# Seven-product stages with an earlier preparation: loads, weight sums, stores and operand splits in another order

## The chip, the cores and the metric

The kernel runs on one core of a Trainium2 chip. TensorE (PE, with its weight load PEld) multiplies, VectorE (DVE), ScalarE (ACT) and GpSimd (POOL) work element by element, and SyncE (SP) issues nearly all the DMAs. Each engine works its own instructions off in order, and so does the queue of SP: an instruction that waits holds up all that stands behind it on its engine. The metric is the device time of one execution in microseconds, of which the median of several runs counts; a profiled execution stands beside it.

## The reference

One layer of an encoder: an input projection into attention and state-space channels, attention, a bidirectional state-space scan, a GLU, an output projection with residual, and a gated embedding with a last norm. The part that the change is about comes behind the attention:

```python
glu = y_ssm @ w_glu[i] + b_glu[i]
y_ssm = glu[..., :D_SSM] * jax.nn.sigmoid(glu[..., D_SSM:])
y_ssm = y_ssm * jax.nn.silu(gate_s)
h = h + jnp.concatenate([y_attn, y_ssm], axis=-1) @ w_out[i]
gate = jax.nn.sigmoid(rms_norm(h, norm_ple[i]) @ w_ple_gate[i])
h = h + gate * (p[i] @ w_ple_proj[i])
return rms_norm(h, norm_final)
```

All matrices are 1024 or 2048 wide, there are 1024 tokens, and everything is float32.

## The kernel before

Every float32 operand is split into a high part H and a low part L (`split`, L306 on: ACT writes H with a cast, L310, DVE writes L with a subtraction, L311), and one product block takes three matmuls of 128 x 512: H times H, H times L, L times H.

Three **stages** follow the attention: stage 0 is the GLU projection (`u_glu`), stages 1 and 2 are the attention half and the state-space half of the output projection (`u_out`). Each has 8 **units** of two 128-wide output tiles. A unit computes its 2 x 2 block product by a scheme with seven block **products** instead of eight: 7 products x 4 blocks of k x 3 matmuls = 84 matmuls of 128 x 512. This costs additions on both sides:

- On the weight side four raw blocks A11, A12, A21, A22 (tiles `sraw`, 6 buffers, loaded by `sw_dma`) give S1 = A21 + A22 and S2 = S1 - A11 (tiles `wraw`), A11 - A21 and A12 - S2 in place. These four sums per unit run on POOL (`sw_sum`, L436). `sw_prep` splits the weights of one product into `wH`, `wL` (4 buffers each). `sw_next` does so ahead of use: before the matmuls of product g it prepares up to product g + 2.
- On the operand side `t_make` forms four sums of the stage's 1024-token inputs, k by k, on POOL (L1127 to L1133), in a background thread: loads to `zz` and `t4` (tile `t` in the trace), 20 steps of waiting, four subtractions, three steps, stores to scratch `d_t`. `put_product` then loads the 28 operand tiles `st` of the next stage during the last unit of a stage, four behind each product, since the 33 large buffers leave only five free beside a full set. Each load is followed some steps later by its split (`fill`, ACT then DVE), one per step.
- On the output side the seven sums are folded into tiles `cx`. `u_out` loads two tiles of 512 KB (x or the sum so far, L1238) at the start of its unit, adds products held in `tz` to them on POOL (L1242), and adds the product in PSUM on DVE in `done` (L1245). In stage 2 each finished half is also squared on ACT and summed on POOL into `xsq` (L1253, L1254). `later` stores the two tiles (L1183). There are four `cx` buffers, that is two units.

The order of everything is the order in which the code issues it (`tc.manual_schedule`). A **step** is one `tick`: four in each product, one behind the three matmuls of a k block. Each tick advances every background thread once and issues at most one waiting fill:

```python
for g in list(self.bgs):
    ...next(g)...
if self.fq and self.fq[0][0] <= self.nt:
    self.fill(*self.fq.pop(0)[1:])
```

Behind the stages the gate (`gate`) multiplies by `w_ple_gate` and `w_ple_proj` in two halves of the tokens; `h_rstd` forms the norm for it, `finish` scales and stores the output of a half.

## Time and profile before

| what | value |
|---|---|
| median of 3 runs | 2205.79 us (2204.56 to 2208.52) |
| the profiled execution | 2209.37 us, span 2207.6 us |
| PE busy | 2093.2 us, 95% of the span, 10140 matmuls |
| PEld busy | 1725.1 us, 78% |
| DVE busy | 1484.1 us, 67% |
| POOL busy | 961.1 us, 44% |
| ACT busy | 798.6 us, 36% |
| DMA | 296.48 MB, mean 134 GB/s |

The span counts from the first to the last instruction; the execution's own time is 1.8 us longer. Busy shares are averages over parts with different limits. A busy PE need not run at its peak: the granted clock and the distance from one matmul's start to the next tell that. The stages lie between 1226 and 1763 us of the span, the gate behind them.

### The profile page before, as it was taken

The numbers are of one execution on the slowest core, as the hardware profiler recorded it, in microseconds if no ns is written. First come the engines' busy times: TensorE is split into PE (matmuls) and PEld (weight loads), VectorE is DVE, ScalarE is ACT, GpSimd is POOL, SyncE is SP. The second block draws the span as 40 slices with busy tenths as digits, with TensorE's granted clock in tenths as the row PEclk, the third lists the DMA queues.
The fourth block names the chain that finished last, engine by engine and source line by source line (L and its number), as shares of the span: only waits on it lengthen the run. The fifth ranks groups of instructions, "written<-read, shape, count | busy, mean of one in ns | idle before, by whom it ended". The sixth has DMA issues, their size and how long they took to land. (4 is left out here: it accounts for less than half of the span.)

```text
span 2207.6 us, 29212 instructions
## 1 busy us (share of the span) xinstructions
PE 2093.2 (95%) x10140; PEld 1725.1 (78%) x10140; DVE 1484.1 (67%) x2394; ACT 798.6 (36%) x1454; POOL 961.1 (44%) x837
## 2 busy tenths in 40 slices
PE   8999999999999999989999899889899899999996
PEld 6888878888878887878888678667677678877885
DVE  7654777688887887749999766736755644455334
ACT  7111222222222222457777423412433433343332
POOL 0234446555655555414212576457578711211222
PEclk9999999999999999999999999889999999999998
DMA  6323232323323223563213564665744444355433
GB/s 210 95 94 102 85 97 80 96 83 100 95 82 107 80 81 103 171 203 134 96 58 100 177 205 148 241 207 197 274 138 157 169 141 127 124 185 170 124 113 124
DMA packets 187732, 296.48 MB, mean 134 GB/s; under 512 B 28864, under 2 KB 79168, under 8 KB 187328
## 3 DMA queue, kind: packets, MB, share of 16 engines
q1 hardware_dynamic: 186432, 292.51, 41.5%
q8 instruction: 80, 1.31, 0.3%
q10 hardware_dynamic: 1152, 2.10, 0.2%
q14 instruction: 68, 0.56, 0.1%
HBM read 211.37 MB, written 77.92 MB: 131 GB/s over the span
## 5 line engine op out<-in xcount | busy, mean ns | idle before, releaser
L311 DVE TENSOR_TENSOR wL<-wraw,wH 128x512 fp32r<-128x512 f32 (+1 forms) x352 | 303.1, 878 | 368.1 <-ACT wH L310 366.3
L310 ACT CAST wH<-wraw 128x512 fp32r<-128x512 f32 (+1 forms) x352 | 205.5, 597 | 356.8 <-DMA wraw<-in_w_gate_dram 110.3
L1174 PE MATMUL pr<-st,wL 128*128 128x512 f32 x672 | 274.6, 409 | 35.3 <-DVE wL L311 35.2
L1172 PE MATMUL pr<-st,wH 128*128 128x512 f32 x672 | 268.9, 400 | 12.2 <-ACT wH L310 12.2
L1173 PE MATMUL pr<-st,wH 128*128 128x512 f32 x672 | 267.7, 398 | 0.0
L1291 PE MATMUL pg<-st,wH 128*128 128x512 f32 x512 | 203.7, 398 | 9.1 <-ACT wH L310 7.7
L1292 PE MATMUL pg<-st,wH 128*128 128x512 f32 x512 | 202.4, 395 | 0.6 <-DVE st L314 0.6
L1293 PE MATMUL pg<-st,wL 128*128 128x512 f32 x512 | 201.6, 394 | 0.7 <-DVE wL L311 0.7
L1174 PEld LDWEIGHTS pr<-st,wL 128*128 128x128 f32 x672 | 130.1, 194 | 81.7 <-DVE wL L311 55.5
L1319 POOL TENSOR_TENSOR h<-cx,tz 128x512 f32<-128x512 f32 x31 | 40.4, 1304 | 309.4 <-DVE tz L1317 309.4
L1172 PEld LDWEIGHTS pr<-st,wH 128*128 128x128 f32 x672 | 130.5, 194 | 40.7 <-ACT wH L310 15.1
L1173 PEld LDWEIGHTS pr<-st,wH 128*128 128x128 f32 x672 | 129.9, 193 | 28.2
L311 DVE TENSOR_TENSOR wL<-sraw,wH 128x512 fp32r<-128x512 f32 x120 | 119.1, 993 | 39.1 <-ACT wH L310 38.5
L1242 POOL TENSOR_TENSOR cx<-cx,tz 128x512 f32<-128x512 f32 x64 | 97.0, 1531 | 107.6 <-DVE tz L1266 45.6
L892 ACT COPY ks<-kp 16x224 f32<-16x224 f32 x32 | 10.7, 335 | 344.0 <-DVE ks L891 216.3
L1291 PEld LDWEIGHTS pg<-st,wH 128*128 128x128 f32 x512 | 97.4, 190 | 32.1 <-ACT wH L310 9.3
L1292 PEld LDWEIGHTS pg<-st,wH 128*128 128x128 f32 x512 | 97.6, 191 | 23.1 <-DVE st L314 2.5
L1293 PEld LDWEIGHTS pg<-st,wL 128*128 128x128 f32 x512 | 97.4, 190 | 22.8 <-DVE wL L311 2.5
L765 POOL TENSOR_TENSOR tab<-pa 128x512 f32<-128x512 f32 x32 | 41.3, 1292 | 156.5 <-DVE r L900 156.5
L574 PE MATMUL zga<-hH,wH 128*128 128x512 f32 x256 | 104.1, 407 | 0.0
L574 PE MATMUL zq<-hH,wH 128*128 128x512 f32 x256 | 102.8, 402 | 0.0
L574 PE MATMUL zgs<-hH,wH 128*128 128x512 f32 x256 | 102.5, 400 | 0.0
(370 smaller groups left out, 5362.1 us busy)
## 6 DMA issues: line engine op xcount, KB each, us to landing
wraw<-in_w_in_dram SPq DMA_DIRECT2D x144, 256.0 KB
wraw<-in_w_gate_dram SPq DMA_DIRECT2D x128, 256.0 KB
sraw<-in_w_out_dram SPq DMA_DIRECT2D x64, 256.0 KB
st<-d_t SPq DMA_DIRECT2D x48, 256.0 KB
sraw<-in_w_glu_dram SPq DMA_DIRECT2D x32, 256.0 KB
cx<-in_xT_dram SPq DMA_DIRECT2D x16, 512.0 KB
d_p<-cx SPq DMA_DIRECT2D x16, 512.0 KB
cx<-d_p SPq DMA_DIRECT2D x16, 512.0 KB
```

The costliest lines, as they stand in the source:

```text
L310: nc.scalar.copy(H, src)
L311: nc.vector.tensor_tensor(L, src, H.bitcast(F32), ALU.subtract)
L574: nc.tensor.matmul(ps[h], H[:, kk, :], rH[:, s], start=(k == 0), stop=False)
L765: gp.tensor_tensor(out, x[:, :, None, :].to_broadcast(sh), pw[:, :, :, None].to_broadcast(sh), ALU.mult)
L1172: nc.tensor.matmul(ps, H[:, k], x[0], start=(k == 0), stop=False)
L1173: nc.tensor.matmul(ps, H[:, k], x[1], start=False, stop=False)
L1174: nc.tensor.matmul(ps, L[:, k], x[0], start=False, stop=(k == 3))
L1242: nc.gpsimd.tensor_tensor(x[:, h], x[:, h], u, ALU.add)
L1291: nc.tensor.matmul(ps, H[:, k % 4], x[0], start=(k == 0), stop=False)
L1292: nc.tensor.matmul(ps, H[:, k % 4], x[1], start=False, stop=False)
L1293: nc.tensor.matmul(ps, L[:, k % 4], x[0], start=False, stop=(k == nk - 1))
L1319: eng.tensor_tensor(hp, ho, t, ALU.add)
```

## The change

- **Weights.** `sw_next` prepares up to product g + 3 instead of g + 2. The sums S1, S2 move from the split of product 1 to that of product 0, A11 - A21 from 2 to 1, A12 - S2 from 3 to 2. The loads of the next unit's first two blocks move from `sw_prep` 0 to 3, those of the other two from 4 to 5.
- **Outputs.** The thread of the next unit starts (and so loads its `cx` tiles) behind product 3 of the unit ahead of it. The addition in `done` runs as a thread (`close`), three steps behind; the stores wait 8 steps instead of 2, the last multiplication's store in `u_glu` five instead of two.
- **Operands.** Between the start of the stages and their end a fill is issued in three of five steps (`paced`). `t_make` loads and stores two tiles of 128 x 1024 where it had four of 128 x 512, waits 14 steps for its loads, and stores 8 steps behind its last subtraction; for stage 2 it begins at unit 1 of stage 1, not at unit 0.
- **Gate.** Behind the stages all threads run out before the last two operand loads; the first gate weights are loaded behind products 3 and 5 and two are split. `h_rstd` waits two steps more. In `finish` the first half's outputs go out every second step, each stored four steps later.

```diff
@@ tick
-        if self.fq and self.fq[0][0] <= self.nt:
+        if self.fq and self.fq[0][0] <= self.nt and (not self.paced or self.nt % 5 in (0, 2, 4)):
@@ sw_prep
         if i == 0:
-            self.sw_dma(u + 1, (0, 1))
-        elif i == 1:
             self.sw_sum(u, S1, A21, A22, ALU.add)
             self.sw_sum(u, S2, S1, A11, ALU.subtract)
-        elif i == 2:
+        elif i == 1:
             self.sw_sum(u, A11, A11, A21, ALU.subtract)
             del self.sr[A21]
+        elif i == 2:
+            self.sw_sum(u, A12, A12, S2, ALU.subtract)
+            del self.sr[S2]
         elif i == 3:
             del self.sr[A11]
-            self.sw_sum(u, A12, A12, S2, ALU.subtract)
-            del self.sr[S2]
+            self.sw_dma(u + 1, (0, 1))
         elif i == 4:
             del self.sr[S1]
-            self.sw_dma(u + 1, (2, 3))
         elif i == 5:
             del self.sr[A12]
-        elif i == 6:
+            self.sw_dma(u + 1, (2, 3))
+        else:
             del self.sr[A22]
@@ sw_next
-        for j in range(g, g + 3):
+        for j in range(g, g + 4):
@@ unit
-        next(thread)
         for i in range(7):
...
             thread.send(ps)
+            if i == 3 and nxt is not None:
+                next(nxt)
             hook(i)
@@ u_out
         def done(x, h, ps):
+            self.bg(close(x, h, ps))
+
+        def close(x, h, ps):
+            for _ in range(3):
+                yield
             nc.vector.tensor_tensor(x[:, h], ps, x[:, h], ALU.add)
...
-        self.bg(self.later(2, (dst[2 * m], r[0])))
+        self.bg(self.later(8, (dst[2 * m], r[0])))
         ps = yield
         done(r[1], h0, ps)
-        self.bg(self.later(2, (dst[2 * m + 1], r[1])))
+        self.bg(self.later(8, (dst[2 * m + 1], r[1])))
@@ finish
             if hf == 0:
+                self.bg(self.later(4, (self.out[n][:, self.half(hf)], hs[n])))
                 yield
-            eng = nc.scalar if hf == 1 and n % 2 else nc.sync
+                yield
+                continue
+            eng = nc.scalar if n % 2 else nc.sync
@@ back
-                if s == 2 and i == 5:
-                    self.w_end = len(self.wq)
-                    self.w_dma()
-                    self.w_dma()
-                elif s == 2 and i == 6:
-                    self.w_split()
+                    elif i == 3:
+                        self.w_end = len(self.wq)
+                        for _ in range(2):
+                            self.w_dma()
+                    elif i == 5:
+                        self.w_dma()
+                        for _ in range(2):
+                            self.w_split()
...
-                        self.bg(self.t_make(1, src, self.four_sm, 20))
-                if u == 0 and s == 1:
-                    self.bg(self.t_make(2, self.d_ms, self.four_sm, 20))
+            if u == 1 and s < 2:
+                self.bg(self.t_make(s + 1, stages[s + 1][0], self.four_sm, 14, 8))
...
-        for _ in range(3):
+        while self.bgs:
             self.tick()
```

The order on the queue of SP in stage 1, one unit while `t_make` runs. Before (`d_t`, `zz`, `t`, `d_ms` belong to `t_make`, `d_p` is the store of finished tiles, `sraw` are weight loads):

```order
L1138 DMA d_t_1_203<-zz 128x512 x2
L1138 DMA d_t_1_203<-t_13708 128x512 x2
L1124 DMA zz<-d_ms_156 128x512 x2
L1124 DMA t_13869<-d_ms_160 128x512 x2
L1183 DMA d_p_164<-cx 128x1024
L1238 DMA cx<-in_xT_dram 128x1024 x2
L1183 DMA d_p_165<-cx 128x1024
L429 DMA sraw<-in_w_out_dram 128x512 x4
```

And now:

```order
L1129 DMA zz<-d_ms_155 128x1024
L1129 DMA t_13843<-d_ms_159 128x1024
L429 DMA sraw<-in_w_out_dram 128x512 x2
L1189 DMA d_p_164<-cx 128x1024
L429 DMA sraw<-in_w_out_dram 128x512 x2
L1189 DMA d_p_165<-cx 128x1024
L1244 DMA cx<-in_xT_dram 128x1024 x2
L1144 DMA d_t_1_203<-zz 128x1024
L1144 DMA d_t_1_203<-t_13843 128x1024
```

The loads of `cx` stood directly behind `t_make`'s stores and loads and were for the unit then beginning; now they stand ahead of those stores and are for the unit behind, and the weight loads go two by two around the stores.

The order on POOL in a unit of stage 2, from the sum S1 (`wraw<-sraw`) of one unit to that of the next. Before:

```order
L436 TENSOR_TENSOR wraw<-sraw 128x512
L436 TENSOR_TENSOR wraw<-wraw,sraw 128x512
L1254 TENSOR_TENSOR xsq<-xsq,tq 128x512
L436 TENSOR_TENSOR sraw<-sraw 128x512
L1242 TENSOR_TENSOR cx<-cx,tz 128x512
L436 TENSOR_TENSOR sraw<-sraw,wraw 128x512
L1254 TENSOR_TENSOR xsq<-xsq,tq 128x512
L1242 TENSOR_TENSOR cx<-cx,tz 128x512 x3
L1254 TENSOR_TENSOR xsq<-xsq,tq 128x512 x2
```

And now:

```order
L436 TENSOR_TENSOR wraw<-sraw 128x512
L436 TENSOR_TENSOR wraw<-wraw,sraw 128x512
L1248 TENSOR_TENSOR cx<-cx,tz 128x512
L436 TENSOR_TENSOR sraw<-sraw 128x512
L1265 TENSOR_TENSOR xsq<-xsq,tq 128x512
L436 TENSOR_TENSOR sraw<-sraw,wraw 128x512
L1265 TENSOR_TENSOR xsq<-xsq,tq 128x512 x2
L1248 TENSOR_TENSOR cx<-cx,tz 128x512
L1265 TENSOR_TENSOR xsq<-xsq,tq 128x512
L1248 TENSOR_TENSOR cx<-cx,tz 128x512 x2
```

The twelve instructions are the same. S1 and S2 stood at product 6 of the unit ahead, A11 - A21 and A12 - S2 at products 0 and 1 of the unit that needs them; now all four stand at products 4, 5 and 6 of the unit ahead.

The order on ACT at the change from stage 0 to stage 1 (`st` are operand fills, `wH` weight casts). Before:

```order
L310 CAST wH<-sraw 128x512
L310 CAST st<-st 128x512 x4
L310 CAST wH<-sraw 128x512
L310 CAST st<-st 128x512 x4
L1221 ACTIVATE tz<-tz,vec 128x512
L310 CAST wH<-wraw 128x512
L310 CAST st<-st 128x512 x4
L1258 COPY tz<-pr 128x512
```

And now:

```order
L310 CAST wH<-wraw 128x512
L310 CAST st<-st 128x512 x2
L1227 ACTIVATE tz<-tz,vec 128x512
L310 CAST wH<-sraw 128x512
L310 CAST st<-st 128x512 x2
L1269 COPY tz<-pr 128x512
L310 CAST wH<-wraw 128x512
L310 CAST st<-st 128x512 x3
```

Four fills stood between two weight casts; now there are two or three, and they reach further into the first unit of the new stage.

## Rows read from the trace of the kernel before

**Rows 1.** Stretches: length, busy us (count) of PE, PEld, DVE, ACT, POOL; clock; DMA
```profile
1226.19:1394.87 168.68, 157.79 (x674) 126.12 (x673) 121.20 (x154) 59.72 (x105) 92.80 (x62) 0.99 0.58 196
1394.87:1582.44 187.57, 166.78 (x673) 131.97 (x674) 109.94 (x141) 52.98 (x96) 113.05 (x79) 0.94 0.63 215
1582.44:1762.70 180.26, 164.38 (x673) 127.52 (x671) 118.41 (x142) 67.42 (x119) 139.08 (x93) 0.96 0.51 171
1335.81:1373.89 38.08, 38.08 (x170) 31.54 (x168) 25.57 (x33) 11.51 (x20) 18.40 (x13) 1.00 0.43 144
1762.70:1786.00 23.30, 16.55 (x65) 12.21 (x65) 12.28 (x28) 9.57 (x17) 5.48 (x4) 0.85 0.51 164
```

**Rows 2.** What PE waited for, 1226 to 1786: total us, times, longest
```profile
PE pr L1174 <- DVE wL L311: 35.2, 32, 4.9
PE pr L1172 <- ACT wH L310: 12.2, 6, 2.8
PE pg L1291 <- ACT wH L310: 4.2, 1, 4.2
```

**Rows 3.** Timeline of PE, stage 1 unit 2: start, us, what, idle before
```profile
1471.18 0.72 PE L1174 MATMUL pr<-st,wL 128*128 128x512 f32 x1 [3.70 <-DVE wL L311]
...
1472.12 0.63 PE L1173 MATMUL pr<-st,wH 128*128 128x512 f32 x1
1472.55 0.63 PE L1174 MATMUL pr<-st,wL 128*128 128x512 f32 x1
```

**Rows 4.** Timeline of POOL in the same unit
```profile
1459.85 1.30 POOL L436 TENSOR_TENSOR sraw<-sraw 128x512 f32<-128x512 f32 x1
1468.09 1.26 POOL L1242 TENSOR_TENSOR cx<-cx,tz 128x512 f32<-128x512 f32 x1 [6.95 <-DMA cx<-in_xT_dram]
1469.31 1.27 POOL L436 TENSOR_TENSOR sraw<-sraw,wraw 128x512 f32<-128x512 f32 x1
```

**Rows 5.** Timeline of SP's queue in the same unit
```profile
1457.19 0.79 SPq L1138 DMA_DIRECT2D d_t<-t  x2
...
1461.34 1.65 SPq L1238 DMA_DIRECT2D cx<-in_xT_dram  x2
```

**Rows 6.** Stretches of the three stages by units, columns as in rows 1
```profile
1226.19:1250.40 24.21, 20.48 (x87) 15.39 (x85) 19.56 (x29) 12.61 (x22) 6.63 (x4) 1.00 0.63 220
1250.40:1335.81 85.41, 80.03 (x338) 63.60 (x336) 58.28 (x68) 23.24 (x40) 61.13 (x43) 0.98 0.59 198
1373.89:1394.87 20.98, 19.20 (x85) 15.59 (x84) 17.79 (x27) 12.35 (x23) 6.64 (x5) 1.00 0.74 256
1394.87:1425.64 30.77, 24.67 (x84) 18.55 (x85) 27.67 (x34) 13.41 (x25) 15.03 (x11) 0.83 0.58 208
1425.64:1524.38 98.74, 84.64 (x337) 66.25 (x336) 44.58 (x57) 18.22 (x32) 67.14 (x49) 0.93 0.61 206
...
1562.46:1582.44 19.98, 19.39 (x86) 15.62 (x85) 14.75 (x23) 11.89 (x23) 7.21 (x5) 1.00 1.02 362
1582.44:1613.40 30.96, 22.25 (x85) 16.96 (x84) 25.58 (x33) 12.82 (x25) 19.57 (x11) 0.89 0.55 196
1613.40:1736.34 122.94, 119.41 (x506) 93.22 (x505) 70.95 (x84) 41.01 (x73) 104.33 (x72) 1.00 0.46 150
1736.34:1762.70 26.36, 22.72 (x85) 17.34 (x83) 21.88 (x25) 13.60 (x23) 15.18 (x10) 0.87 0.67 239
```

**Rows 7.** Timeline of DVE, stage 2: a split beside POOL, one alone
```profile
1644.89 1.45 DVE L311 TENSOR_TENSOR wL<-wraw,wH 128x512 fp32r<-128x512 f32 x1 [1.26 <-ACT wH L310]
...
1646.86 0.68 DVE L311 TENSOR_TENSOR wL<-sraw,wH 128x512 fp32r<-128x512 f32 x1
```

**Rows 8.** Timeline of POOL, stage 2, a sum beside a split
```profile
1642.43 1.75 POOL L436 TENSOR_TENSOR sraw<-sraw,wraw 128x512 f32<-128x512 f32 x1
```

**Rows 9.** Chain that ended last: start, us, landing of a 512 KB store
```profile
1410.13 2.80 DMA d_ms<-cx
```

**Rows 10.** What PE waited for, 1990 to 2040 (second gate half)
```profile
PE pg L1291 <- ACT wH L310: 3.5, 2, 2.7
```

94 lines of the change are left out of this document (49 added, 45 removed).

## The prediction

> **What bounds the kernel now.** I read the stretches of the three stages first [rows 1]. Two units of stage 0 in which PE never idles take 38.08 us, so a unit of 84 matmuls costs 19.04 us at the full clock, and eight cost 152.3. The stages last 168.7, 187.6 and 180.3 us, that is 16.4, 35.2 and 27.9 us more: 79.5 us in all, the most that the stages can give back. The view of PE's waits [rows 2] says for what: 47.4 us are waits for the weight split (35.2 for `wL`, 12.2 for `wH`), in 38 pieces. No operand, no PSUM buffer and no raw load appears there. The rest is mostly the clock: behind a long wait matmuls start every 0.43 us [rows 3], in an undisturbed unit every 0.227 (19.04 / 84); that is 1.2 GHz where 2.4 is granted otherwise, and the granted share in stages 1 and 2 is 0.94 and 0.96 [rows 1]. If c is the mean share, 2(1 - c) of a stretch runs at half rate and half of that is lost: 0.06 x 187.6 + 0.04 x 180.3 + 0.01 x 168.7 = 20 us. Twelve more lie in the gaps around each wait. A stall that is removed thus gives back more than one and a half times its listed wait.
>
> Next, where the units lose it [rows 6]: unit 0 of stage 0, 5.2; its units 1 to 4, 85.4 - 76.2 = 9.2; the change to stage 1 (last unit and first), 51.75 - 38.1 = 13.7; units 1 to 4 of stage 1, 98.7 - 76.2 = 22.6; the change to stage 2, 12.9; units 1 to 6 of stage 2, 122.9 - 114.2 = 8.7; its last unit 7.3. This adds up to the 79.6.
>
> Last, who makes the split late. In unit 2 of stage 1 POOL stands 6.95 us in front of an addition to `cx` [rows 4] whose load SP issued at 1461.34, behind `t_make`'s store of 1457.19 [rows 5]. A weight sum (1469.31) is queued behind that addition; its split comes late, and PE waits 3.70 us at 1471.18 [rows 3]. So in units with `t_make` the bound is SP's order, passed on by POOL's order.
>
> **The change part by part.** Matmuls, splits and sums keep their number; the sum is made of waits.
>
> *Loads a pair ahead, sums and stores moved.* The `cx` loads now go out behind product 3 of the unit ahead, 10.9 us into it. They need the buffers of the unit before that, whose second store is issued nine steps of 0.68 us into the unit (6.1) and lands 2.8 us later [rows 9], at 8.9: SP does not wait. Landing 6.7 us after issue (1461.34 to 1468.09) the data are there at 17.6, and POOL wants them at 19.04 + 2.72 + 0.6 = 22.4. The cause of rows 4 goes. The sums stand two products (5.4 us) earlier, so an addition that waits no longer holds a sum that is due. Instead POOL's load comes up: in a unit of stage 2 it works 104.3 / 6 = 17.4 us [rows 6], 1.45 us each for twelve instructions, which at 19.04 leaves 1.6. While `t_make` runs (25 steps a round instead of 26, four subtractions each) it is 8 + 4 x 28/25 = 12.5 instructions, 18.1 us. It fits, barely; a lag of some 4 us is covered, since a sum is done 7 us or so ahead of its product. Upper bound of the gain in units 1 to 4 of stages 0 and 1: 31.8, all. Lower: all POOL instructions as slow as the one beside a split, 1.75 us [rows 8]; then a unit of stage 1 takes 12.5 x 1.75 = 21.9, four lose 11.4, and 20 is gained (in stage 0, with two multiplications in place of four additions, it is 10.5 x 1.75 = 18.4, no loss). The 17.4 is measured in this same mix, so I stay near the upper end and leave one wait with its restart in each stage, 4 together: **28**. In units 1 to 6 of stage 2 nothing but the lateness of the sums causes the 1.4 us a unit: upper bound 8.7; lower 12 x 1.75 = 21.0 against 20.5 now, minus 3; I take **7.7**. What is late next there is nothing that I can see before POOL itself.
>
> The pages know a stricter rule for this place. In the rows a subtraction on DVE takes 0.68 us alone and 1.45 beside POOL [rows 7], POOL's 1.26 alone [rows 4] and 1.75 beside DVE [rows 8]. The Trainium skill, "SBUF — State Buffer", section "Who interferes with whom", has a DVE instruction with two SBUF inputs and a GpSimd instruction that reads SBUF take turns, one blocking the other for its whole length. By the rule a unit of stage 2 would hold 12 x 1.28 + 7 x 0.68 = 20.1 us of turns, one of stage 1 with `t_make` 20.8; the two terms would be 31.8 - 4 x 1.8 = 25 and 6 x 0.4 = 2.3, and the sum 53.6, that is 2152. The trace's 17.4 us, blocked time included, says that most turns are lost by DVE.
>
> *The deeper preparation.* There are still four `wH` and `wL`, so the cast for product g + 3 must wait until PE has left product g - 1. Behind it on ACT and DVE are queued fills, squares and the additions from PSUM; these wait for PE's latest products anyway, and PE needs the split three products, 8.2 us, later. Cost nothing as long as ACT and DVE together are less than some 6 us behind; at a change of stage that cover is thin. The later `done` keeps a PSUM buffer one product longer of the three that four buffers allow: nothing.
>
> *Unit 0 of stage 0.* Its last operands still arrive from `d_t` behind the last attention store; only the weight casts overtake the fills. Between 0 and 5.2, taken **2.7**.
>
> *The changes of stage.* In the two changes DVE works 17.8 + 27.7 = 45.5 and 14.8 + 25.6 = 40.3 us [rows 6] where PE needs 38.1. The pacing removes none of that. It spreads 28 fills over 47 steps, from about step 6 of the last unit to step 53, and the last operand is needed at step 52 to 55: the weight casts no longer stand behind bursts of four fills, but the fills come just in time. What DVE has too much, 7.4 + 2.2 = 9.6, stays, and I add 2.7 a change for a restart at the half clock (13 matmuls x 0.2): 15 of 26.6 left, **11.6** gained. Bounds: 0 (fills late instead of weights) and 24.
>
> *The end.* The last unit loses 7.3 to 14 fills in bursts; I leave 3. Behind it PE is busy 16.55 of 23.30 us [rows 1]: 4.2 of the idle time are the first gate weight [rows 2], which is now split during product 5, the rest the wait of `h_rstd`, which gets two more steps (2.7 us). But the last two operands need the last stores of `cx`: landed 2.8 us after the last addition and loaded again (6.7 us at most, as a `cx` load), they were hidden behind the 4.2. They come 9.5 us behind the stages, and their blocks of k are due 14 x 0.68 = 9.5 us into the gate, splits still to do: I charge 3. Together 4.3 + 6.75 - 3 = **8**, bounds 2 and 14. In the gate's second half PE waits 3.5 us for weights [rows 10] while SP stores the first half's outputs one per step; at half the pace, with the restarts, **4** (0 to 5).
>
> Sum: 28 + 7.7 + 2.7 + 11.6 + 8 + 4 = 62. The profiled execution takes 2209.4, 3.6 above the median of the runs, and shows no wait that the others would lack, so I take the sum from the median: 2205.8 - 62 = **2144**.
>
> **The rivals.** *The pace undoes itself.* Fills due at steps 51 to 53 for a product that begins at step 52 make PE wait for operands in the first units. For it: DVE's 45.5 us; against: DVE has slack in the unit behind. Without the 11.6 and the 4.3 of the last unit: 2160.
>
> *POOL paces the units.* With 1.75 us an instruction the two terms become 20 and minus 3: a gain of 43, 2163. For it: DVE will run denser beside POOL; against: the measured 1.45.
>
> *The `cx` loads turn into a ring.* An addition, its store (9 steps, 2.8 us), the load behind it and the next addition but one now hang together over two units. It decides from the landing time: up to 11 us POOL waits for nothing; at 17.4 it waits 6 a unit, as in rows 4, and with 18 us of work a unit takes 25. Sixteen units of `u_out` are then 400 us instead of 367.8; with some 20 saved elsewhere: 2218. For it: DMA engines busy 1.02 in the change of stage [rows 6]; against: 0.46 to 0.74 in the other stretches.
>
> *The change does not reach what it aims at*: some other wait, of SP above all, stands behind each removed one. Then about 2204.
>
> **How the numbers follow.** Forecast (2128 to 2158) 0.64; pace 0.14; POOL 0.10; the ring 0.06; no effect 0.06. The range reaches from 2128, since not all upper bounds (sum 89) come together, to 2178, where the first two rivals come together (62 - 15.9 - 18.7 = 27): left out are the ring, no effect, and a little below. A measurement tells 0.2% (4.4 us) from no change: faster 0.88, same 0.05, slower 0.07.
>
> **What would show it.** Right: units 1 to 6 of stages 1 and 2 at 19.0 to 19.5 us; no wait of POOL for `cx` above 1 us; PE's waits for `wL` from 35 to under 15 us, left in the first unit of stages 1 and 2; the clock share of stage 1 at 0.97 or more. Wrong: waits of PE for `st`, which means pace; POOL busy over 95% of the units, which means the shared port; POOL waiting for `cx<-in_xT_dram` or `cx<-d_p`, the ring.

## The result, and the profile after

The changed kernel takes 2174.9 us (median of four runs, 2171.96 to 2179.83) against 2206.0 (2204.56 to 2208.52): a ratio of 0.986, 95% interval 0.9837 to 0.9883, or 31 us less. The forecast was 2144, 62 us less: faster, as it said, by half as much. The profiled execution takes 2172.48 us with a span of 2170.6, against 2209.37 and 2207.6. The first is the second lowest of the changed kernel's four runs, and the other lies above all four of the kernel before, so the two traces lie 37.0 us apart, not 31. The accounts below are of the traces.

The stretches of the changed kernel, as in [rows 1] and [rows 6]: length, busy us (count) of PE, PEld, DVE, ACT, POOL; clock; DMA share, GB/s. In order: unit 0 of stage 0; units 1 to 3; its last unit; the first unit of stage 1; units 1 to 6; the last; the first unit of stage 2; units 1 to 3; 4 to 6; the last; the entry of the gate.

```profile
1226.80:1254.52 27.72, 21.28 (x86) 15.81 (x85) 22.63 (x30) 13.03 (x23) 11.07 (x8) 0.94 0.73 266
1254.52:1313.37 58.85, 58.85 (x254) 48.54 (x252) 38.45 (x48) 17.15 (x29) 39.52 (x28) 0.97 0.55 189
1370.49:1389.53 19.04, 19.04 (x86) 15.77 (x84) 17.10 (x24) 12.27 (x23) 8.47 (x5) 1.00 0.82 278
1389.53:1418.23 28.70, 22.21 (x85) 14.92 (x84) 27.27 (x35) 12.49 (x24) 12.35 (x8) 1.00 0.70 246
1418.23:1534.11 115.88, 115.88 (x505) 95.78 (x504) 69.83 (x85) 28.92 (x49) 95.45 (x66) 0.99 0.72 238
1534.11:1553.15 19.04, 19.04 (x85) 15.77 (x84) 17.72 (x25) 9.95 (x18) 11.07 (x7) 1.00 0.85 301
1553.15:1587.02 33.87, 24.29 (x86) 16.95 (x84) 29.63 (x34) 14.93 (x28) 19.45 (x13) 0.88 0.55 196
1587.02:1645.17 58.15, 58.15 (x254) 48.04 (x252) 33.38 (x41) 20.26 (x35) 45.16 (x31) 0.98 0.50 163
1645.17:1705.67 60.50, 58.93 (x254) 46.71 (x252) 36.67 (x42) 19.54 (x35) 51.55 (x36) 1.00 0.50 161
1705.67:1729.53 23.86, 20.10 (x85) 15.29 (x83) 16.38 (x20) 13.07 (x22) 15.36 (x12) 1.00 0.58 198
1729.53:1760.00 30.47, 21.12 (x78) 14.42 (x78) 18.54 (x35) 11.46 (x20) 8.90 (x6) 0.83 0.35 117
```

What is to be seen: the long middle of the stages runs at PE's pace (115.88 for six units, 58.15 for three), and the last units of stages 0 and 1 take 19.04. The three first units take 27.72, 28.70 and 33.87, and in those of stages 1 and 2 DVE is busy 27.27 and 29.63 us.

What PE waits for, 1200 to 1790 (total us, times, longest), beside [rows 2]; under it the line of the kernel before for the norm's matmul `bc`, which [rows 2] do not have:

```profile
PE pr L1177 <- DVE st L311: 15.6, 16, 2.4
PE pr L1176 <- DVE cx L1256: 7.9, 7, 3.1
PE pg L1302 <- ACT wH L310: 7.9, 2, 6.9
...
PE pr L1176 <- ACT st L310: 3.6, 3, 1.7
PE bc L358 <- DVE tq L352: 0.8, 1, 0.8
```

```profile
PE bc L358 <- DVE tq L352: 2.6, 1, 2.6
```

The waits for weight halves (47.4 us before) are gone but for 0.5 us. In their place stand waits for operands `st` (L310, L311; 19.2 us), for a PSUM buffer that an addition in `close` (L1256) has to free, and for the first gate weight. Of the 7.9 us for PSUM, 1.5 lie in units 4 to 6 of stage 2 and 3.7 in its last unit; the rest is in the two changes. The losses against 19.04 us a unit, from the starts of the 84 matmuls of each unit:

| place | before | after | gain forecast | gain measured |
|---|---|---|---|---|
| units 1 to 6 of stages 0 and 1 | 31.8 | 3.4 | 28 | 28.4 |
| units 1 to 6 of stage 2 | 8.7 | 4.4 | 7.7 | 4.3 |
| unit 0 of stage 0 | 5.2 | 8.7 | 2.7 | -3.5 |
| the two changes (last and first unit) | 26.6 | 24.5 | 11.6 | 2.1 |
| last unit, and the gate's entry | 7.3; 27.3 us for 82 matmuls | 4.8; 30.5 us for 78 | 8 | 2.5 and -4 |
| rest of the gate | 400 us for 1695 matmuls | 393 us for 1701 | 4 | 8 |
| ahead of the stages | 1226.2 | 1226.8 | 0 | -0.6 |

This adds up to 37. In the gate the same 839 matmuls of the last part take 193.0 us now and took 200.0. Two stretches of the kernel before, its entry and that part, and under them the part in the changed kernel:

```profile
1762.70:1790.00 27.30, 20.55 (x82) 15.47 (x82) 14.56 (x32) 13.06 (x21) 5.48 (x4) 0.87 0.53 165
...
1990.00:2190.00 200.00, 192.53 (x839) 156.82 (x838) 84.45 (x132) 65.81 (x115) 37.84 (x29) 0.99 0.39 123
```

```profile
1960.00:2153.00 193.00, 190.00 (x839) 156.03 (x837) 84.09 (x131) 65.59 (x115) 37.88 (x29) 1.00 0.40 128
```

### The profile page after: what moved, and what is told of

It is laid out like the page before. It is cut to its first block, busy times and chain, and to the rows that moved or that the text cites. A ratio compares the mean times of both kernels' runs of the same rounds, so it can differ in the third digit from the quotient of the medians.

```text
span 2170.6 us, 29380 instructions
## 1 busy us (share of the span) xinstructions
PE 2076.4 (96%) x10140; PEld 1717.4 (79%) x10140; DVE 1496.1 (69%) x2394; ACT 798.7 (37%) x1454; POOL 965.1 (44%) x837
## 3 DMA queue, kind: packets, MB, share of 16 engines
q1 hardware_dynamic: 181824, 292.51, 41.5%
## 5 line engine op out<-in xcount | busy, mean ns | idle before, releaser
L311 DVE TENSOR_TENSOR wL<-wraw,wH 128x512 fp32r<-128x512 f32 (+1 forms) x352 | 305.3, 884 | 360.5 <-ACT wH L310 355.2
L310 ACT CAST wH<-wraw 128x512 fp32r<-128x512 f32 (+1 forms) x352 | 205.3, 598 | 344.1 <-DMA wraw<-in_w_gate_dram 98.1
L1178 PE MATMUL pr<-st,wL 128*128 128x512 f32 x672 | 265.3, 395 | 0.2
L1177 PEld LDWEIGHTS pr<-st,wH 128*128 128x128 f32 x672 | 127.8, 190 | 49.0 <-DVE st L311 23.2
L1176 PEld LDWEIGHTS pr<-st,wH 128*128 128x128 f32 x672 | 127.9, 190 | 44.6 <-issue 8.7
L311 DVE TENSOR_TENSOR wL<-sraw,wH 128x512 fp32r<-128x512 f32 x120 | 120.2, 1002 | 41.2 <-ACT wH L310 41.1
L1248 POOL TENSOR_TENSOR cx<-cx,tz 128x512 f32<-128x512 f32 x64 | 102.1, 1606 | 64.5 <-DVE tz L1277 54.6
L310 ACT CAST wH<-sraw 128x512 fp32r<-128x512 f32 x120 | 73.0, 616 | 94.2 <-PE pr L1177 59.7
```

The source lines that it names most:

```text
L310: nc.scalar.copy(H, src)
L311: nc.vector.tensor_tensor(L, src, H.bitcast(F32), ALU.subtract)
L1176: nc.tensor.matmul(ps, H[:, k], x[0], start=(k == 0), stop=False)
L1177: nc.tensor.matmul(ps, H[:, k], x[1], start=False, stop=False)
L1178: nc.tensor.matmul(ps, L[:, k], x[0], start=False, stop=(k == 3))
L1248: nc.gpsimd.tensor_tensor(x[:, h], x[:, h], u, ALU.add)
```

## The experiments

All are edits of the changed kernel, except e4, an edit of the kernel before. e2, e5 and e13 leave a part of the computation out, so their times belong to no kernel that could be used. Times are medians, ratios those to the kernel before on the same chip, with 95% intervals. The start of the stages scatters between 1225.7 and 1235.2 us over the profiled executions, so causes are read from each trace's own losses (us over 19.04 a unit; "change" is the last unit and the first of the next stage; "entry" runs from the start of the last unit of stage 2 to the gate's first `bc` matmul, L358, which stands two steps, 12 matmuls or 2.7 us, earlier in the order of the kernel before):

| kernel | time | ratio | unit 0 | 0: 1-6 | change to 1 | 1: 1-6 | change to 2 | 2: 1-6 | last unit | entry |
|---|---|---|---|---|---|---|---|---|---|---|
| before | 2206.0 | 1 | 5.2 | 9.3 | 13.7 | 22.6 | 12.9 | 8.7 | 7.3 | 47.5 |
| after | 2174.9 | 0.9860 (0.9837-0.9883) | 8.7 | 1.7 | 9.7 | 1.6 | 14.8 | 4.4 | 4.8 | 51.9 |
| e1 | 2170.4 | 0.9834 (0.9812-0.9857) | 3.0 | 6.2 | 9.7 | 0.2 | 6.4 | 7.8 | 6.2 | 51.7 |
| e2 | 2149.6 | 0.9742 (0.9718-0.9766) | 4.9 | 1.7 | 0 | 0 | 0 | 3.9 | 6.2 | 51.8 |
| e3 | 2181.6 | 0.9883 (0.9860-0.9906) | 10.6 | 1.3 | 11.3 | 2.4 | 12.8 | 8.1 | 4.0 | 51.5 |
| e4 | 2189.4 | 0.9918 (0.9894-0.9941) | 4.5 | 4.4 | 14.2 | 7.7 | 11.8 | 8.5 | 7.1 | 48.5 |
| e5 | 2171.1 | 0.9826 (0.9812-0.9839) | 9.0 | 2.5 | 7.1 | 1.8 | 10.2 | 5.0 | 7.4 | 51.9 |
| e6 | 2176.5 | 0.9852 (0.9835-0.9869) | 9.8 | 2.6 | 10.2 | 2.1 | 13.9 | 4.6 | 7.3 | 51.9 |
| e7 | 2170.4 | 0.9821 (0.9808-0.9835) | 8.9 | 2.0 | 9.9 | 1.6 | 14.8 | 0.9 | 0.6 | 47.2 |
| e8 | 2175.1 | 0.9844 (0.9830-0.9857) | 10.2 | 2.1 | 10.1 | 1.8 | 14.8 | 4.3 | 4.7 | 51.3 |
| e9 | 2177.9 | 0.9852 (0.9829-0.9874) | 10.2 | 1.6 | 10.4 | 1.2 | 14.8 | 5.7 | 6.2 | 48.3 |
| e10 | 2163.7 | 0.9795 (0.9772-0.9818) | 10.1 | 2.6 | 10.1 | 0 | 9.7 | 0 | 0.9 | 46.3 |
| e11 | 2173.4 | 0.9842 (0.9815-0.9868) | 4.3 | 3.3 | 7.3 | 3.1 | 6.1 | 9.5 | 6.4 | 52.8 |
| e12 | 2159.6 | 0.9774 (0.9750-0.9798) | 2.3 | 5.9 | 9.7 | 0.5 | 6.5 | 1.8 | 3.1 | 46.7 |
| e13 | 2154.8 | 0.9760 (0.9739-0.9781) | 6.2 | 1.7 | 2.7 | 0 | 3.8 | 3.7 | 6.3 | 52.1 |
| e14 | 2179.2 | 0.9870 (0.9848-0.9892) | 10.0 | 1.6 | 9.8 | 1.5 | 14.8 | 4.1 | 4.7 | 49.1 |
| e15 | 2158.4 | 0.9770 (0.9746-0.9794) | 3.2 | 4.8 | 8.9 | 0 | 6.1 | 0.6 | 0.8 | 45.2 |
| e16 | 2151.7 | 0.9743 (0.9722-0.9765) | 3.6 | 5.2 | 8.8 | 0.3 | 6.0 | 0.7 | 0.9 | 41.5 |
| e17 | 2155.5 | 0.9767 (0.9753-0.9781) | 4.5 | 4.4 | 8.9 | 0 | 6.2 | 0.6 | 0.9 | 41.5 |
| e18 | 2151.0 | 0.9746 (0.9726-0.9765) | 2.4 | 5.4 | 9.7 | 0 | 6.4 | 0 | 0.8 | 42.0 |

### The middle of the stages: the loads (e4)

```diff
@@ unit (kernel before): the thread is started behind product 3 of the unit ahead
-        next(thread)
         for i in range(7):
...
             thread.send(ps)
+            if i == 3 and nxt is not None:
+                next(nxt)
```

> The kernel before with one part of the change: the thread of the next unit starts, and so loads its two cx tiles, behind product 3 of the unit ahead. Weight sums, look-ahead, stores, additions, pace and gate stay as before. Prediction's reading (SP's order, handed on by POOL's addition that waits for cx, is what makes the weight splits late in units 1 to 4): units 1 to 4 of stage 1 fall from 98.7 to about 80 us, those of stage 0 from 85.4 to 78; time 2206 - 25 = about 2181. Rival (the weight sums were simply too close to their split, and the loads are covered anyway): units 1 to 4 stay within 4 us, time 2200 or more.

Measured: 2189.4. Units 1 to 6 of stage 1 fall from 22.6 to 7.7 us, those of stage 0 from 9.3 to 4.4, others stay. POOL's waits in units 1 to 4 of stage 1, first of the kernel before, then of e4:

```profile
POOL cx L1242 <- DMA cx<-in_xT_dram: 21.1, 3, 8.3
```

```profile
POOL cx L1243 <- DVE tz L1267: 11.6, 3, 4.3
```

The 21.1 us of waiting for the loads, one of which is in [rows 4], are gone, with 19.8 of the 28.4 us gained in these units. The expected 25 was too much: the other 8.6 need the rest of the change. In stage 2, where the loads were not late, the 8.7 stays. So the prediction's reading of SP's order holds, and is worth about two thirds of the term. Which part of the change gave the other 8.6 no run separates.

### Stage 2: PSUM waits, and who causes them (e3, e7, e10)

In units 4 to 6 of the changed kernel's stage 2 PE waits for PSUM. One unit there, on POOL, ACT and DVE (timeline: start, us, instruction, idle before and its releaser):

```profile
1676.39 1.73 POOL L1248 TENSOR_TENSOR cx<-cx,tz 128x512 f32<-128x512 f32 x1
1680.08 1.30 POOL L1265 TENSOR_TENSOR xsq<-xsq,tq 128x512 f32<-128x512 f32 x1 [1.96 <-ACT tq L1264]
1682.60 3.40 POOL L1248 TENSOR_TENSOR cx<-cx,tz 128x512 f32<-128x512 f32 x2 [1.23 <-DVE tz L1277]
...
1679.30 0.63 ACT L1264 ACTIVATE tq<-cx 128x512 f32<-128x512 f32 x1 [3.68 <-DVE cx L1256]
1679.84 1.65 ACT L310 CAST wH<-sraw 128x512 fp32r<-128x512 f32 x3
...
1678.59 0.68 DVE L1256 TENSOR_TENSOR cx<-pr,cx 128x512 f32<-128x512 f32 x1
1679.19 0.68 DVE L1274 TENSOR_TENSOR tz<-pr,tz 128x512 f32<-128x512 f32 x1
1680.48 1.45 DVE L311 TENSOR_TENSOR wL<-sraw,wH 128x512 fp32r<-128x512 f32 x1 [0.61 <-ACT wH L310]
```

The addition on DVE (1678.59) releases ACT's square (1679.30), which stood 3.68 us at the head of ACT's queue; three weight casts behind it come only at 1679.84, and POOL has stood 1.96 us in front of the sum of squares. POOL's 17.2 us of work (51.55 / 3) with these stops make a round of 20.7 us.

e3 takes the change's delay of the additions away:

```diff
         def close(x, h, ps):
-            for _ in range(3):
-                yield
             nc.vector.tensor_tensor(x[:, h], ps, x[:, h], ALU.add)
```

(`done` then adds at once, with no thread.)

> The changed kernel with the additions from PSUM issued at once behind their product, as before the change, not three steps later. Theory L (the three steps hold the PSUM buffer too long; together with squares and sums that lag they make PE wait 7.9 us for PSUM, units 4 to 6 of stage 2): those waits go, stage 2 falls from 176.4 to about 172, time about 2170. Rival (POOL and ACT are behind in stage 2 in any case, and DVE's queue stands behind what waits for them): the waits for PSUM turn into waits for the weight halves and stage 2 stays at 176 or grows to 180; time 2174 or more.

Measured: 2181.6, units 1 to 6 of stage 2 lose 8.1 instead of 4.4 (of the 7.9 us that the expectation puts into units 4 to 6, only 1.5 lay there). PE waits for no addition in `close` any more, but for the weight half (1200 to 1790):

```profile
PE pr L1178 <- DVE wL L311: 4.3, 9, 0.7
```

The delay helps; the theory that it is the cause falls.

e7 takes work from POOL:

```diff
-                nc.gpsimd.tensor_tensor(acc, acc, s2, ALU.add)
+                eng = nc.vector if x is r[1] else nc.gpsimd
+                eng.tensor_tensor(acc, acc, s2, ALU.add)
```

> The changed kernel with two of the four additions to xsq in each unit of stage 2 (those of the second tile) on DVE instead of POOL: POOL has 10 instructions a unit there instead of 12. Theory Q (the PSUM waits in units 4 to 6 of stage 2 come from POOL: 17.2 us of work and some 3 us of waits for ACT's squares and DVE's sums make a round of 20.7 us, more than PE's 19.04): units 4 to 6 go to 19.0 to 19.2 and the wait of the last unit shrinks; time 2166 to 2171. Rival (DVE's order is what is late: the addition from PSUM stands behind a weight half that waits for ACT): DVE gets two more instructions, units 4 to 6 stay at 20.5 or grow; time 2174 to 2180.

Measured: 2170.4; units 4 to 6 at 19.04, the last unit loses 0.6 instead of 4.8. So the round through POOL is what paces these units. e10 leaves all work where it is and takes only the square out of the way:

```diff
             nc.vector.tensor_tensor(x[:, h], ps, x[:, h], ALU.add)
             if not sq:
                 return
+            for _ in range(6):
+                yield
             acc = self.xsq[:, h]
```

> The changed kernel with the squares (and the sums of xsq behind them) of stage 2 issued six steps behind the additions instead of at once. Theory A (in the first unit of stage 2 ACT stands 5.4 and 8.7 us in front of a square that waits for an addition of DVE, with the casts of operands that PE needs queued behind it; that is why this first unit loses 14.8 us where that of stage 1, which has no squares, loses 9.7): the first unit of stage 2 falls from 33.9 to 27 to 29 us, time 2168 to 2171. Rival D (DVE is full there in any case, and ACT waits because DVE is behind): the first unit stays over 32 us, time 2173 to 2176.

Measured: 2163.7, more than expected. Units 1 to 6 lose nothing, the last 0.9, and the first unit of stage 2 takes 28.78 us instead of 33.87. ACT's waits in that first unit, in the changed kernel and in e10:

```profile
ACT xsq L1261 <- DVE cx L1256: 14.1, 2, 8.7
ACT wH L310 <- POOL wraw L436: 5.7, 1, 5.7
```

```profile
ACT wH L310 <- POOL wraw L436: 14.1, 2, 8.4
ACT xsq L1263 <- DVE cx L1256: 1.5, 1, 1.5
```

In the changed kernel ACT stands 14.1 us in front of two squares, with casts of operands that PE needs behind them. In e10 it stands 14.1 us in front of weight casts, for POOL's sums, and their products come three later. POOL has the same 12 instructions a unit in e10 and keeps pace: it was not too much work but the stops that squares put into the round.

### The first units: pace or DVE's work (e1, e11, e2, e13, e5, e6)

```diff
@@ e1
-        self.paced = True
+        self.paced = False
@@ e11
-        ... self.nt % 5 in (0, 2, 4)
+        ... self.nt % 5 != 3
@@ e2: fill of a stage's operand (e13: for k 2 and 3 only)
-            self.split(x[:, 0], x[:, 1], x[:, 1].bitcast(F32), gain)
+            self.nc.scalar.copy(x[:, 0], x[:, 1].bitcast(F32))
```

> The changed kernel with the operand splits issued one per step throughout, as before the change; all else stays. Theory P (the pace itself makes the first unit of a stage wait: a split issued in three of five steps comes just ahead of its matmul, and DVE has time to spare): the first units of stages 1 and 2 fall from 28.7 and 33.9 us towards 21, unit 0 of stage 0 from 27.7 towards 24, last units stay near 19 to 20; time about 2155 to 2160, and PE's waits for the operand (15.6 us) go. Theory D (DVE has more work in the two units of a change than PE, 44.4 and 47.4 us against 38.1, whoever issues it when): the waits only change place, back to the weight halves wL and into the last units; the two units of a change stay within 2 us of 47.7 and 57.7 in sum, time 2168 to 2182.

> The changed kernel with operand splits issued in four of five steps instead of three. The 28 splits are then issued by step 6 + 35 = 41 of the change, where the last is needed at step 52 to 55; with three of five it was step 53. Theory P for the late products (the last two products of a first unit take 5 to 10 us instead of 2.7 because their splits are issued just ahead of them): products 5 and 6 of the first units come down to 2.7 to 4; unit 0 of stage 0 loses 3 to 5 instead of 8.7, the first unit of stage 2 some 7 to 10 instead of 14.8. Theory D for the sum (DVE's 44 us of work): the first unit of stage 1 still loses 8 to 10, now in its first products. Time 2163 to 2170. If the loss in all first units were DVE's alone: 2173 to 2177.

> The changed kernel, where the splits of the stages' operands write the high half only: DVE's subtraction for the low half is left out there (28 for each of the three stages), so that part of the computation is missing; ACT's cast, the loads, the pace and all matmuls stay. Theory D: DVE loses 28 x 0.6 to 1.6 us = 17 to 44 us of work in each change, falls well below 38 us, and the first units of stages 1 and 2 go to 19 to 21 us; PE's waits for operands nearly vanish; time 2174.9 - 9.7 - 12 - some 3 in stage 0 = about 2150. Theory P: the casts still come at the same steps, just ahead of the matmuls; first units stay over 24 us, time above 2163.

> The changed kernel, in which the low half of the stages' operands is left out in blocks of k 2 and 3: DVE's subtraction is missing in 14 of the 28 splits of each stage (that part of the computation is missing). Casts, loads, pace and matmuls stay. Theory D (the first unit of stage 1 is as long as DVE's work with its waits in the change, 44.4 + 3.2 us, less the last unit's 19.04): with 14 x 0.65 to 1 us less it is 34 to 38 us, no more than PE's 38.1, and the first unit of stage 1 loses under 2 us, that of stage 2 under 5 (its squares stay). Theory P (late splits make late products): products 5 and 6 of the first units still take 4 to 7 us each, stage 1 loses 4 to 6. Time by D 2153 to 2159, by P 2162 to 2167.

The two units of the change to stage 1 (changed kernel, e1, e11, e13, e2, in this order; columns as above):

```profile
1370.49:1418.23 47.74, 41.25 (x169) 30.69 (x168) 44.37 (x58) 24.76 (x46) 20.82 (x12) 1.00 0.74 259
```

```profile
1372.88:1420.66 47.78, 41.39 (x169) 31.65 (x168) 43.47 (x58) 25.02 (x46) 17.14 (x11) 0.96 0.72 246
```

```profile
1373.07:1418.42 45.35, 39.84 (x170) 31.07 (x168) 42.01 (x58) 24.75 (x46) 16.56 (x10) 1.00 0.75 260
```

```profile
1370.14:1410.96 40.82, 38.98 (x169) 31.18 (x168) 34.72 (x44) 24.86 (x46) 17.38 (x12) 1.00 0.87 302
```

```profile
1373.51:1411.59 38.08, 38.08 (x170) 31.53 (x168) 24.49 (x30) 24.87 (x46) 17.06 (x13) 1.00 0.91 320
```

As long as all 58 DVE instructions are there, the two units last as long as DVE is busy plus 3.3 to 4.3 us, at each of the three paces. With 44 they last 40.8, with 30 exactly PE's 38.08. For stage 1 DVE's work decides, as theory D had it: 7.0 of the 9.7 us go with half of the subtractions, the rest with the other half. The 2.7 left in e13 lie in products 5 and 6 (3.56 and 4.61 us for 2.72), the two that the pace makes late; theory P may have that much, but no run takes the pace away with half of the subtractions.

Elsewhere the pace has more. Unit 0 of stage 0 loses 8.7 with three of five, 4.3 with four, 3.0 without a pace; its products 5 and 6 take 5.04 and 9.05, 3.14 and 6.58, 3.61 and 3.60. With 12 subtractions left out at the same pace it loses 4.9 (e2; the 28 of the expectation hold for stages 1 and 2). What a late split stands behind there, the changed kernel's rows of ACT and PE say:

```profile
1244.28 0.62 ACT L310 CAST wH<-sraw 128x512 fp32r<-128x512 f32 x1 [3.60 <-DMA sraw<-in_w_glu_dram]
1244.80 1.65 ACT L310 CAST st<-st 128x512 fp32r<-128x512 f32 x3
...
1245.47 0.50 PE L1176 MATMUL pr<-st,wH 128*128 128x512 f32 x1 [1.37 <-ACT st L310]
```

A weight cast of the next unit waits 3.60 us for its raw block, three operand casts stand behind it, and PE waits for the first of them.

The change to stage 2 loses 14.8 with three of five, 6.1 with four and 6.4 without a pace. Its row in the changed kernel, then in e1:

```profile
1534.11:1587.02 52.91, 43.33 (x170) 32.73 (x168) 47.35 (x58) 24.88 (x46) 30.52 (x19) 0.92 0.66 234
```

```profile
1534.84:1579.34 44.50, 40.34 (x170) 32.41 (x169) 42.65 (x56) 23.83 (x44) 22.86 (x14) 0.96 0.80 278
```

There pace, squares and DVE's work meet: splits that are still to be issued stand behind squares, and the squares wait for additions of DVE. Later squares gain 5.1 (e10), a quicker pace 8.4 to 8.7, both together (e15: 6.1) no more than the pace; and with the pace and the squares as they are but DVE's subtractions left out, nothing is lost (e2). Theory D holds for the change to stage 1 and falls here: in e1 these two units went from 52.9 us (the 57.7 in the expectation adds the wrong units) to 44.5. But with a quicker pace units 1 to 6 lose more (8 us in stages 0 and 2 of e1, of which stage 1 gives back 1.4; 8 in all three of e11), so that e1 comes out in theory D's range for another reason than D's, and e11, whose first units lose as little as was expected or less, gains 1.5 us, less than its noise, where 5 to 12 were expected.

e5 and e6 ask what POOL costs DVE in a change:

```diff
@@ sw_sum, e5: left out for these units; e6:
-        self.nc.gpsimd.tensor_tensor(self.sr[o], self.sr[a], self.sr[b], op)
+        eng = self.nc.vector if u in (7, 8, 15, 16) else self.nc.gpsimd
+        eng.tensor_tensor(self.sr[o], self.sr[a], self.sr[b], op)
```

> The changed kernel, in which the weight sums of POOL are left out in the last and the first unit of a stage (units 7, 8, 15 and 16 of 24, four sums each; blocks that are there stand in for the sums, so those products are not the ones of the computation). All of DVE's 58 instructions in a change stay. In the changed kernel DVE is busy 44.4 us there, 0.77 us an instruction, where instructions that follow each other without POOL beside them start 0.60 us apart, which would be 35 us. Theory C (contention: what DVE has too much in a change is the lengthening beside POOL, some 9 us): with 8 of POOL's 12 instructions gone, DVE's mean falls below 0.70 us, the first unit of stage 1 from 28.7 to 20 to 23 us, that of stage 2 from 33.9 to 24 to 28; time 2155 to 2163. Theory N (58 instructions on DVE's one queue are too many, with their waits for ACT and PE, whatever POOL does): first units within 2 us of now, time 2170 or more.

> The changed kernel with the weight sums of units 7, 8, 15 and 16 done by DVE instead of POOL. Nothing is left out. DVE has 8 instructions more in a change (about 8 x 0.6 to 0.68 = 5 us) and POOL 8 fewer. Theory C (each POOL instruction beside a saturated DVE costs DVE about 0.77 us, more than DVE would need for the same sum): DVE 66 x 0.63 = 42 us in a change instead of 44 to 47; first units 1 to 5 us shorter, time 2163 to 2173. Theory N (DVE's count decides): first units 4 to 5 us longer each, time 2180 to 2186.

The change to stage 1, first in e5, then in e6:

```profile
1375.32:1420.45 45.13, 40.94 (x170) 31.68 (x168) 40.59 (x58) 24.87 (x46) 12.18 (x7) 0.97 0.78 274
```

```profile
1371.41:1419.67 48.26, 41.27 (x169) 30.67 (x168) 43.62 (x64) 24.76 (x46) 12.93 (x7) 1.00 0.74 256
```

Of POOL's sums five are gone here and not eight, since a unit's sums are done in the unit ahead. Five fewer shorten the same 58 DVE instructions by 44.37 - 40.59 = 3.8 us, 0.76 each, and the losses of the two changes by 2.6 and 4.6 us: contention is there, more than the 2 us a unit of theory N, but not the 9 us that theory C asked for, and the time is theory N's. Done on DVE, the sums cost what they cost beside it (44.37 and 43.62): e6 is where it was, and neither theory's number came. The saturated DVE is not relieved here by moving these sums between it and POOL.

### The gate's entry (e8, e9, e14)

ACT, POOL and PE behind the stages in the changed kernel:

```profile
1735.36 0.63 ACT L1264 ACTIVATE tq<-cx 128x512 f32<-128x512 f32 x1 [6.06 <-DVE cx L1256]
1735.90 1.12 ACT L310 CAST wH<-wraw 128x512 fp32r<-128x512 f32 x2
...
1729.14 5.04 POOL L1248 TENSOR_TENSOR cx<-cx,tz 128x512 f32<-128x512 f32 x3 [3.22 <-DVE tz L1277]
...
1736.55 0.79 PE L1302 MATMUL pg<-st,wH 128*128 128x512 f32 x1 [6.86 <-ACT wH L310]
```

POOL's last three additions end at 1734.2, an addition of DVE follows, then ACT's square; the first gate weights stand behind that square.

```diff
@@ e8 (e14: both splits and the load behind product 4)
-                    elif i == 5:
-                        self.w_dma()
-                        for _ in range(2):
-                            self.w_split()
+                    elif i == 4:
+                        self.w_split()
+                    elif i == 5:
+                        self.w_dma()
@@ e9, e14: t are the cx tiles of the last unit
-        self.put_h(hg, 0, [14, 15], wait=3)
+        for j, t in zip((14, 15), self.last):
+            x = self.hl("st")
+            self.split(x[:, 0], x[:, 1], t[:, self.half(0)], self.g_ple[:, j : j + 1])
+            hg[j] = (x[:, 0], x[:, 1])
```

> The changed kernel with the first gate weight split behind product 4 of the last unit and the second left to the gate, instead of both behind product 5: there the cast stands in ACT's queue behind a square that waits 6.06 us for POOL's last additions, and PE waits 6.86 us for it. Theory G (that queue position is the whole loss at the gate's entry): the wait of 6.86 us goes and the time falls by 5 to 7, to 2168 to 2170. Rival T (the last two operands of the gate come from the last stores in any case, so PE waits for them at block 14 instead): DVE's last additions come some 3 to 4 us earlier, since they no longer stand behind the weight halves, and only that is gained: 2170 to 2173.

> The changed kernel, in which the gate's last two operands (14 and 15) are split from the cx tiles of the last unit in SBUF, not loaded back from memory behind the last stores. Theory T (at the gate's entry PE is bound by this round trip: last addition at 1741.0, store issued at 1740.5 and load at 1743.3, split at 1751.8 to 1753; the earlier split of the first weight gained nothing for that reason): the split comes 7 to 9 us earlier, PE passes block 14 without a stop, and the time falls by 5 to 9, to 2166 to 2170. Rival W (the gate's own weights and the norm are as late: the third and fourth weight are cast at 1741.7 and 1750.4): the wait turns into waits for wH, gain under 3, time 2172 to 2175.

> The changed kernel with both edits at the gate's entry: the first two gate weights are split behind product 4 of the last unit, and the last two operands are split from SBUF. Theory H (the two bounds hide each other: without the wait for the first weight PE reached block 14 before its operand, and with the operand it had waited for the weight already): from the start of the last unit to the end 464.9 falls to 456 to 459, time 2167 to 2170. Rival: a third bound (DVE's weight halves stand behind the operand splits and the last additions, which wait for POOL) leaves 461 to 464, time 2171 to 2175.

(In e9 and e14 `u_out` keeps its last two tiles in `self.last`.) Measured: the entry, 51.9 us, becomes 51.3, 48.3 and 49.1; the times are 2175.1, 2177.9 and 2179.2, outside all the expected ranges; in the traces of e9 and e14 the stages begin at 1233.1 and 1233.9 us, 6 to 7 later than in the changed kernel, so the entry itself is what tells. In e9 PE passes block 14 without a stop, but a wait of 5.4 us for the first weight stays. The stretch from the start of the last unit to the end, 464.9 us, takes 464.8, 461.7 and 464.0 (2177.6 - 1713.6), where theory H asked for 456 to 459. PE's waits in the entry of e14:

```profile
1741.00 0.79 PE L1305 MATMUL pg<-st,wL 128*128 128x512 f32 x1 [3.01 <-DVE wL L311]
1752.29 2.08 PE L345 MATMUL cs<-ones,xsq 128*128 128x1 f32 x16 [3.14 <-POOL xsq L1266]
```

In e14 both edits took their own wait away, and most of it came back elsewhere: at the low half of the weight (DVE works off the gate's operands first) and at the norm's column sums, which wait for POOL's last sum of squares. Theory H falls; the rival, a third bound, holds. That all of this is late by one backlog, of POOL, DVE and ACT at the end of stage 2, is argued and not shown: with less of it (e7, e10) the entry takes 47.2 and 46.3, but 4.2 and 3.9 us of that gain are the last unit's own, and behind later squares and a quicker pace the two edits are worth 3.7 (e15 to e16: 45.2 to 41.5), not much more than the 2.8 of e14.

### Together (e12, e15, e16, e17, e18)

e12 is e1 with e7 and e9; e15 is e10 with e11; e16 adds both gate edits to e15; e17 adds to e16

```diff
-                self.bg(self.t_make(s + 1, stages[s + 1][0], self.four_sm, 14, 8))
+                self.bg(self.t_make(s + 1, stages[s + 1][0], self.four_sm, 10, 15))
```

and e18 is e17 without a pace.

> The changed kernel with three edits together: operand splits one per step (no pace), two of four xsq additions of a unit on DVE, the gate's last two operands split from SBUF. If the causes are separate: minus 4.5 for the pace, minus 4.5 for the xsq additions (and 4 more, since without the pace the PSUM waits of stage 2 were 7.5 us), minus 5 to 9 for the gate: 2153 to 2161. If the gate's gain falls away: 2162 to 2166. If what one edit frees is taken by the next (DVE above all): over 2167.

> The changed kernel with the squares six steps later and operand splits in four of five steps. If the two are separate causes: later squares keep units 1 to 6 of stage 2 at 19.04, first units lose about 4.3, 7.3 and 5 to 6 us (10.1, 10.1 and 9.7 with later squares alone), units 1 to 5 of stages 0 and 1 some 5 more than now; time 2155 to 2160. If the pace's gain is eaten by waits for weight halves in the units behind: 2161 to 2165.

> All together: the changed kernel with later squares, splits in four of five steps, both gate weights split behind product 4 and the last two operands split from SBUF. If the gate's two edits gain 6 to 9 on top of later squares and pace: 2147 to 2152. If later squares have already removed the wait at the gate's entry (there the first weights were cast 16 us earlier than in the changed kernel, and PE waited 4.9 us for their low half): 2152 to 2158.

> The version with later squares, splits in four of five steps and the two gate edits, with t_make's rounds made as long as a unit (28 steps) and its four subtractions put at steps 10 to 13 of each unit, where they now drift through it in rounds of 25. Theory R (units 1 to 4 of stage 0 lose 5.2 us to a ring of POOL and DVE: t_make's four subtractions stand ahead of the multiplication L1221, DVE's product L1224 waits for that with a weight half behind it, and POOL's next multiplication waits for DVE; one round takes 20.0 us): these units go to 19.04 to 19.3, time 2146 to 2149. Rival (the ring is as long wherever the four stand, since POOL has to do them within the unit): no change, 2150 to 2154.

> As the last one, with one split per step instead of four in five. If the sum of DVE's work decides the first units, whatever the pace: within 3 us of the last one. If splits that come still earlier help unit 0 of stage 0 and the first unit of stage 2 further: 2 to 4 us faster. If bursts of splits push the weight halves back, as in the kernel before: 3 to 6 us slower.

Measured: 2159.6, 2158.4, 2151.7, 2155.5 and 2151.0: e12, e15 and e16 in the ranges for separate causes. Two of these are partly luck: e12's entry, 46.7 us, is 0.5 below that of e7, where 5 to 9 were asked of the gate's edit, and e16 lies at the edge of its range, with 3.7 us at the entry where 6 to 9 were asked for. e16 beats both kernels: it is 57 us below the kernel before on its chip (2208.4) and some 23 below the changed one. e17 and e18 add nothing that the intervals could tell from e16. In e17 units 2 to 5 of stage 0 still lose 1.0 us each where they were to be clean, so the place of `t_make`'s subtractions is not the cause; what makes these units 20.0 us long with a quicker pace, while three of five leaves them clean, stays open. e18 shows that, with the squares later, the pace hardly matters for the sum: unit 0 gains 2.1 on e17, the change to stage 1 loses 0.8.

## Why the prediction was right, and where it was wrong

The direction was right and the size was not: 2174.9 lies outside the 2128 to 2158 of the forecast. It lies among the times that the prediction kept for its first two rivals together, but not for their reasons: the pace took its toll in part, and POOL's two terms did not fall to 20 and minus 3 (28.4 and 4.3 were measured). What failed is the terms for the changes of stage, for unit 0 of stage 0, and for the last unit with the gate's entry.

**Right: the loads.** The term of 28 measured 28.4, units 1 to 6 of stage 1 run at 19.04 but for 1.6 us, POOL waits for no `cx` load in them, and the clock of those units is 0.99. e4 shows the mechanism for 19.8 of it. No rival came of it: neither POOL's pace in stages 0 and 1 nor the ring of loads.

**Wrong: the changes of stage, 11.6 forecast, 2.1 measured.** The change to stage 1 went as forecast: 7.4 of DVE's excess and 2.7 for a restart were to stay, 10.1, and 9.7 did, but that the sum agrees is partly luck: 6.3 are DVE's work over PE's 38.1, 3.4 are times in which DVE itself waits, and the clock is 1.00 in both units, so no restart at the half clock is among them. What failed is the change to stage 2: 2.2 and 2.7 were to stay, and 14.8 did. The 2.2 came from DVE's 40.3 us in the kernel before; in the changed kernel it is busy 47.35 us of these 52.91 and waits another 5.6. And the pace was taken to cost no more than a restart: it costs 8.4 there (e1), 5.1 of them because splits issued late stand behind squares (e10), and all of it only beside a DVE that is full (e2). So the rival of the pace was right for this change, and not for the other, where the loss is 9.7 at three of five and without a pace (7.3, 8.9 and 8.8 at four of five in e11, e15 and e16). The sign that it named, waits for `st`, does not tell the two apart: PE waits 5.3 us for DVE's `st` in the change to stage 1 too.

**Wrong: unit 0 of stage 0, 2.7 forecast, -3.5 measured.** The step weighed only that weight casts overtake the operand splits; the pace was not costed for this unit at all, and costs 5.7 (e1). DVE has room there (22.63 of 27.72 us); what the pace does is to leave casts for PE's products 5 and 6 behind a weight cast that waits for its raw block (the rows above). It is not the pace alone: with 12 subtractions fewer the unit loses 4.9 at the same pace (e2).

**Half right: units 1 to 6 of stage 2, 7.7 forecast, 4.3 measured.** The sums come earlier and the 1.4 us a unit go, as said, until the round through POOL, ACT and DVE has fallen behind; units 4 to 6 then lose 3.4. "What is late next there is nothing that I can see before POOL itself" was the failed sentence. POOL's work, 17.4 us a unit, was nearly right (17.2); what was not counted was that POOL also waits for squares, and these for DVE's additions, so that the round takes 20.7 (e7 and e10 bring these units to 19.04). That the later `done` costs nothing was not what failed, although PE now waits for PSUM: without it these units lose more (e3).

**Wrong: the gate's entry.** 8 was forecast for the last unit and the entry together: 2.5 came in the last unit and the entry lost some 4. The first weight was split earlier in the code, but behind a square on ACT: the queue that it was moved past was read, the one that it was moved into was not. Its wait grew from 4.2 us to 6.9, while the wait for the norm fell from 2.6 to 0.8, as said. But the square is not the whole of it: with the first weight ahead of it the entry takes 51.3 instead of 51.9 (e8), since the low half of that weight and the next weight (PE waits 3.0 and 4.7 us for them in e8) and, in e14, the norm's column sums (3.1) are as late, and they stand in no term of the sum. Why they are late stays open. The 3 for the last two operands were about right (e9 takes 3.6 off the entry). In its second half the gate gained 7 where 4 was forecast: the wait of [rows 10] went with all of its restart.

Altogether 62 - 9.5 (changes) - 6.2 (unit 0) - 3.4 (stage 2) - 9.5 (last unit and entry) + 4 (rest of the gate) - 0.6 + 0.4 is 37, the difference of the traces.

## What to carry to other kernels

Before a stall is priced, count for the stage the work of the engine that feeds it, with that engine's own waits: where this is more than the bound engine needs, another order only moves the wait. An instruction that waits for a late result (here a square behind a late addition) belongs far enough back in its in-order queue that nothing due stands behind it; six steps were worth 11 us here (14 by the two ratios), more than any other single edit that left no work out. And where removing a wait gains little (0.6 us in e8, of the 6.9 that PE stood there), read what else is as late at that place before the next edit: here the low half of the same weight, the next weight and the norm were.
